# Three small vector operations of a two-branch attention layer go from VectorE to GpSimd

## The chip, the cores and the metric

One NeuronCore of one Trainium2 chip runs the whole kernel. The metric is the device time of one execution in microseconds (us); the lower, the better. The engines are named as the profile names them: PE (TensorE, matrix products), DVE (VectorE), ACT (ScalarE), POOL (GpSimd), SP (the queue that issues the transfers). Each engine works through its own queue in order; engines wait for one another by semaphores.

## What is computed

One encoder layer over a prompt of 2048 frames (and 8 running streams of 16 new frames with 512 cached ones). The rows are normalised and modulated, projected, and go through two attention branches; each branch's output is multiplied by a silu gate, projected, and both are merged. Branch A has 4 heads of differential attention (two softmaxes, the second subtracted with a factor lambda). Branch B has 8 heads of stick-breaking attention, whose weights are a sigmoid times a product of one minus the sigmoids of all later keys. The lines of the reference that the change bears on:

```python
# branch A
p = jax.nn.softmax(jnp.where(mask, s, -jnp.inf), axis=-1)
w = p[:, :, 0] - lam * p[:, :, 1]
# branch B
log_1m = jnp.where(mask, jax.nn.log_sigmoid(-z), 0.0)
log_a = jax.nn.log_sigmoid(z) + lax.cumsum(log_1m, axis=3, reverse=True) - log_1m
a = jnp.where(mask, jnp.exp(log_a), 0.0)
# both
ya = (oa.reshape(b, s, WIDTH_A) * jax.nn.silu(za)) @ w_branch_a
yb = (ob.reshape(b, s, WIDTH_B) * jax.nn.silu(zb)) @ w_branch_b
```

## The kernel before

The work has three stages. Up to about 150 us the inputs are normalised and modulated. Up to about 1745 us follow eight units, 0 to 7: for each of four pairs of heads a unit of branch A (the even ones) and a unit of branch B (the odd ones). After that come the branch outputs, the merge and the output projection, with the streams' attention between them.

A unit takes the 16 prompt tiles of 128 rows in turn, t = 0 to 15. `project` multiplies the tile with the unit's weights, some steps ahead of the attention; `scores` makes the scores of tile t against all keys up to it, in chunks of 512 columns, each in one PSUM bank of three (`ps_s`). The scores of a row lie in segments of at most 1024 keys, so a tile from t = 8 on has two segments. High-precision products are made of a high and a low half in 16 bits, so every operand is cut in two (`split`).

Branch B, per head and chunk, from the last chunk to the first: ACT makes two sigmoids (L135), one into the tile `sc_p` and one in place in the bank. DVE runs a multiplying scan from right to left over the bank into `sc_n` (`stick`, L675), each chunk beginning with the leftmost value of the chunk to its right. Where that chunk lies in the next segment (once for each head of a tile from t = 8 on), DVE first copies that value into the column behind the segment (L674) and the scan begins with the copy. POOL multiplies `sc_p` with `sc_n`, shifted by a column (`stick_weights`, L681), which is why that column must be there. Then `turn`: ACT casts the product to its high half (L609), DVE subtracts to get the low half (L612), and SP issues a transposing transfer into `wt` (L619), from which PE multiplies with the values (L762, L763), a set lag later. In unit 7 the turn follows at once; in the other units it is put off by a lag.

Silu of branch B's gate (`silu`, called at the start of `scores` of each tile): ACT makes the sigmoid of z into a tile of which there is one (`r2`), DVE multiplies z with it in place (L725). The result lies in a ring of eight (four in `szs`, four in `gt`) until POOL multiplies the head's output with it (`natural`, L745).

Branch A, per tile (`softmax_pair`): DVE takes the scores out of the bank with their maximum (L595), ACT makes the exponentials with their sums (L135), DVE works out factors from the sums (`sums`, L642 to L645): r[:,1] and r[:,2] for the join of both softmaxes (L650), and r[:,0], the common factor, which is scaled at L645 and is not needed before `turn` (ACT's cast L319 and DVE's subtraction L324). POOL applies the rotary embedding to branch A's projections (L507, L509, L512).

What comes when is settled twice: the program is written as interleaved pieces with lags, and a scheduler then orders each engine's queue by its own estimate of durations. So an operation that goes to another engine also moves others.

Of the kernel before, what the change touches and what calls it, by code (L numbers as in the profile page):

```python
# [22 lines left out]
ALU = mybir.AluOpType  # L23
# [102 lines left out]
def layer_kernel(ctx: ExitStack, tc: tile.TileContext, a: dict):  # L126
    nc = tc.nc
    V, S, G, T = nc.vector, nc.scalar, nc.gpsimd, nc.tensor
# [4 lines left out]
    def act(**kw):  # L133

        i = S.activation(**kw)  # L135
        if last_table[0] is not None:
            tc.add_manual_dep(i.ins, last_table[0].ins.name, NOSYNC, reason="table order")
        last_table[0] = i
        return i

    def kept(x):
        tc.keep_in_program_order(x)
        return x
# [68 lines left out]
    def bank(tag, dt=F32):  # L212
        return ps.tile([P, 512 if dt == F32 else 1024], dt, tag=tag, name=f"ps_{tag}", bufs=BANKS[tag])
# [114 lines left out]
    ls = ls_i.bitcast(F32)  # L328
# [244 lines left out]
    def new_job(U, t, c, nb, pool=None):  # L573

        segs = [(0, nb)] if t == NT else [(lo, min(lo + SEG, nb)) for lo in range(0, nb, SEG)]
        return dict(U=U, t=t, c=c, pool=pool, segs=[dict(lo=lo, hi=hi) for lo, hi in segs])
# [9 lines left out]
    def evacuate(job, seg, c, p, lo, n, sc_pos, sc_neg, ch):  # L586

        buffers(job, seg)
        if job["U"]["kind"] == 0:
            if "mx" not in job:  # L590
                job["mx"] = tiny.tile([P, 2, 4], F32, tag="mx", name="mx")
                job["nch"] = 0
            job["nch"] = max(job["nch"], ch + 1)
            dst = seg[("p", "n")[c]]
            V.tensor_scalar(out=dst[:, lo : lo + n], in0=p[:, 0:n], scalar1=sc_pos, scalar2=None,  # L595
                            op0=ALU.mult, op1=ALU.max, accum_out=job["mx"][:, c, ch : ch + 1])
        else:

            act(out=seg["p"][:, lo : lo + n], in_=p[:, 0:n], func=AF.Sigmoid, scale=sc_pos)
            act(out=p[:, 0:n], in_=p[:, 0:n], func=AF.Sigmoid, scale=sc_neg)  # L600

    def turn(job, seg, scale=None):

        nb = seg["hi"] - seg["lo"]
        nk = nb * P
        w16 = seg["n"].bitcast(F16)
        hi, lo, src = w16[:, 0:nk], w16[:, nk : 2 * nk], seg["p"][:, 0:nk]
        if scale is None:
            x = S.copy(out=hi, in_=src)  # L609
            if job["t"] < NT and job["U"]["u"] < 7:  # L610
                kept(x)
            V.tensor_tensor(out=lo, in0=src, in1=hi, op=ALU.subtract)  # L612
        else:
            split(hi, lo, src, scale, S)
        if job["t"] == NT:
            seg["wt"] = job["pool"].tile([P, 10, P], F16, tag="dwt", name="dwt", bufs=2)
        else:
            seg["wt"] = wtp.tile([P, 2 * SEG, P], F16, tag="wt", name="wt", bufs=WT_BUFS)
        nc.sync.dma_start_transpose(out=seg["wt"][:, 0 : 2 * nb, :], in_=w16[:, 0 : 2 * nk])  # L619
        if job["t"] < NT:  # L620
            cost = (PV_A, PV_B)[job["U"]["kind"]]
            for fn in pv(job, seg):
                later_on(PV_LAG, fn, cost)

    def softmax_pair(job):

        segs = job["segs"]
        nm = tiny.tile([P, 2], F32, tag="nm", name="nm")
        V.tensor_reduce(out=nm, in_=job["mx"][:, :, 0 : job["nch"]], axis=AX.X, op=ALU.max, negate=True)
        l = tiny.tile([P, 2, 2], F32, tag="l", name="l")  # L630
        r = tiny.tile([P, 3], F32, tag="r", name="r")
        n_all = sum(seg["hi"] - seg["lo"] for seg in segs) / SEG

        def powers(i, c):
            seg = segs[i]
            w = seg[("p", "n")[c]][:, 0 : (seg["hi"] - seg["lo"]) * P]
            act(out=w, in_=w, func=AF.Exp, bias=nm[:, c : c + 1], accum_out=l[:, c, i : i + 1])

        def sums():
            sums = l[:, :, 0]  # L640
            if len(segs) > 1:
                V.tensor_tensor(out=sums, in0=l[:, :, 0], in1=l[:, :, 1], op=ALU.add)  # L642
            V.reciprocal(out=r[:, 0:2], in_=sums)
            V.scalar_tensor_tensor(out=r[:, 2:3], in0=sums[:, 0:1], scalar=r[:, 1:2], in1=nlam, op0=ALU.mult, op1=ALU.mult)
            V.tensor_tensor(out=r[:, 0:1], in0=r[:, 0:1], in1=ls[:, 0:1], op=ALU.mult)  # L645

        def joined(seg):
            nk = (seg["hi"] - seg["lo"]) * P
            p, n = seg["p"][:, 0:nk], seg["n"][:, 0:nk]
            x = V.scalar_tensor_tensor(out=p, in0=n, scalar=r[:, 2:3], in1=p, op0=ALU.mult, op1=ALU.add)  # L650
            if job["t"] < NT:
                kept(x)

        stages = [(EXP_LAG, lambda i=i, c=c: powers(i, c)) for i in range(len(segs)) for c in range(2)]
        stages.append((EXP_LAG + SUM_LAG + 2.0 * n_all, sums))
        for i, seg in enumerate(segs):
            at = EXP_LAG + SUM_LAG + 2.0 * n_all + i
            stages += [(at, lambda seg=seg: joined(seg)), (at + TURN_LAG, lambda seg=seg: turn(job, seg, r[:, 0:1]))]
        for lag, fn in stages:
            if job["t"] == NT:  # L660
                fn()
            else:
                later_on(lag, fn)

    def stick(seg, later, lo, n, src):

        nk = (seg["hi"] - seg["lo"]) * P
        dst = seg["n"]
        if lo + n == nk and later is None:
            first = 2.0 ** STICK  # L670
        else:
            first = dst[:, lo + n : lo + n + 1]
            if lo + n == nk:
                V.tensor_copy(out=first, in_=later["n"][:, 0:1])  # L674
        V.tensor_tensor_scan(out=dst[:, lo : lo + n][:, ::-1], data0=src[:, 0:n][:, ::-1], data1=zero_t[:, 0:1].to_broadcast([P, n]),  # L675
                             initial=first, op0=ALU.mult, op1=ALU.add)

# [9 lines left out]
    def scores(U, t, jobs):  # L687

        sc, kind = U["sc"], U["kind"]
        nch = t // 4 + 1  # L690
        own = [new_job(U, t, c, t + 1) for c in range(1 + kind)]
        jobs += own

        def chunk(c, ch):
            job = own[c if kind == 1 else 0]
            seg = job["segs"][ch * 4 // SEG]
            n = 512 if ch < t // 4 else (t % 4 + 1) * P
            p = bank("s")
            qst, kk = U["q", t], U["k"][ch]
            diag = ch == t // 4  # L700
            T.matmul(p[:, 0:n], qst[:, c, :], kk[:, c, 0:n], start=True, stop=False)  # L701
            T.matmul(p[:, 0:n], qst[:, 2 + c, :], kk[:, c, 0:n], start=False, stop=not diag)  # L702
            if diag:
                m = mask_a if kind == 0 else mask_b
                T.matmul(p[:, n - m.shape[1] : n], idb, m, start=False, stop=True)  # L705
            evacuate(job, seg, c, p, ch * 512 - seg["lo"] * P, n, sc[:, 3:4], sc[:, 4:5], ch)
            if kind == 0:
                if diag and c == 1:
                    softmax_pair(job)
                return  # L710
            i = job["segs"].index(seg)
            later = job["segs"][i + 1] if i + 1 < len(job["segs"]) else None
            stick(seg, later, ch * 512 - seg["lo"] * P, n, p)
            if ch * 4 == seg["lo"]:
                if later is not None:
                    stick_weights(job, later, None)
                if i == 0:
                    stick_weights(job, seg, later)

        def silu():  # L720

            z = silu_z[t % len(rings)]
            sg = stg.tile([P, 256], F32, tag="r2", name="r2", bufs=1)[:, 0:P]
            act(out=sg, in_=z, func=AF.Sigmoid)
            V.tensor_tensor(out=z, in0=z, in1=sg, op=ALU.mult)  # L725

        order = [(c, ch) for ch in range(nch) for c in range(2)] if kind == 0 else \
                [(c, ch) for c in range(2) for ch in reversed(range(nch))]
        return ([(0.1, silu)] if kind == 1 else []) + [(2.0 if ch < t // 4 else (t % 4 + 1) / 2, lambda c=c, ch=ch: chunk(c, ch)) for c, ch in order]

    def natural(U, t, po, pool=stg):
# [35 lines left out]
    def later_on(lag, fn, cost=0.0):  # L767

        spent[1] += 1
        bisect.insort(due, (spent[0] + lag, spent[1], cost, fn))  # L770
# [276 lines left out]
    with tc.tile_pool(name="p0", bufs=1) as p0:  # L1047
# [28 lines left out]
        first = wide_tile().rearrange("p k n -> p (k n)")  # L1076
# [561 lines left out]
```

## Time and profile before

| what | us |
|---|---|
| median of 3 runs (lowest, highest) | 2212.37 (2209.06, 2217.97) |
| the profiled execution | 2207.3 |
| its span, first to last instruction | 2205.4 |
| PE busy | 2044.0 |
| DVE busy | 1734.5 |
| ACT busy | 1598.9 |
| POOL busy | 726.7 |

The profile is of one execution. Busy time is summed for each engine; a wait is put down to the instruction that ended it. A group has one line of the source, an engine, an operation and a shape, with busy time, mean duration in ns and the idle time ahead of it. A timeline has one instruction in a row: start and duration in us.

### The profile page before, as it was taken

To read this page: it belongs to the slowest core of one execution; us is meant where nothing else is said; L and a number is where in the kernel's file an instruction comes from. 1 tells how busy PE (TensorE), PEld (TensorE's weight loads), DVE (VectorE), ACT (ScalarE), POOL (GpSimd) and SP (SyncE) were. 2 spreads that over 40 slices of the span, in tenths; PEclk is the share of its full clock that TensorE was granted. 3 is DMA by queue.
4 is the path that set the end of the run, shared out by engine and by line. 5 is a ranking of instruction groups with operands and counts; after the bars stand their busy time and mean duration, and the time that the engine had idled before them with its cause. 6 is when DMAs were issued, how large, how long until landed. Compare 5 with 4: busy or idle time off the path is not lost. (4 is left out here: it accounts for less than half of the span.)

```text
span 2205.4 us, 40973 instructions
## 1 busy us (share of the span) xinstructions
PE 2044.0 (93%) x14504; PEld 1091.4 (49%) x14504; DVE 1734.5 (79%) x3651; ACT 1598.9 (72%) x3080; POOL 726.7 (33%) x618
## 2 busy tenths in 40 slices
PE   3999999999999999999999998999997799999997
PEld 1545555555555455555555545455554344444443
DVE  5668868889877887987878887787789778778874
ACT  3977677788877777978687788875687656666641
POOL 0433024466301444742034464402344412112220
PEclk9999999999999999999999999999999899999999
DMA  9778668899797999978888899885777899998862
GB/s 331 259 249 191 132 151 231 184 222 206 199 243 174 221 191 208 214 197 216 204 223 202 186 229 217 216 198 123 171 154 157 204 254 222 245 246 236 227 161 67
DMA packets 820814, 449.96 MB, mean 204 GB/s; under 512 B 551962, under 2 KB 759114, under 8 KB 820096
## 3 DMA queue, kind: packets, MB, share of 16 engines
q1 hardware_dynamic: 819660, 446.96, 82.1%
q8 instruction: 113, 1.85, 0.3%
q14 instruction: 93, 0.76, 0.1%
q10 hardware_dynamic: 948, 0.39, 0.1%
HBM read 229.87 MB, written 86.02 MB: 143 GB/s over the span
## 5 line engine op out<-in xcount | busy, mean ns | idle before, releaser
L681 POOL TENSOR_TENSOR sc_p<-sc_p,sc_n 128x127 f32<-128x127 f32 (+7 forms) x192 | 319.3, 1665 | 557.8 <-DVE sc_n L675 528.4
L466 PEld LDWEIGHTS <-hs 128*128 128x128 f16 x3120 | 292.8, 99 | 316.8 <-issue 9.1
L466 PE MATMUL ps_mm<-wa,hs 128*128 128x512 f16 x1590 | 390.5, 381 | 6.8 <-DMA hs<-hT_d 3.7
L466 PE MATMUL ps_mm<-wb,hs 128*128 128x512 f16 x1530 | 380.9, 380 | 0.0
L675 DVE TENSOR_TENSOR_SCAN sc_n<-ps_s,sc_n,zero_t 128x512 f32<-128x512 f32 x192 | 245.3, 1278 | 40.3 <-ACT ps_s L135 34.5
L612 DVE TENSOR_TENSOR sc_n<-sc_p,sc_n 128x128 f16<-128x128 f32 (+7 forms) x192 | 224.7, 1173 | 39.3 <-ACT sc_n L609 38.5
L701 PE MATMUL ps_s<-k,qst 128*128 128x512 f16 (+3 forms) x640 | 223.1, 349 | 32.2 <-DVE sc_n L675 27.8
L540 PEld LDWEIGHTS <-hs 128*128 128x128 f16 x1632 | 155.3, 98 | 184.2 <-DVE qst L569 4.8
L540 PE MATMUL ps_t<-wa,hs 128*128 128x512 f16 x1020 | 243.4, 381 | 1.1 <-DVE qst L569 0.7
L135 ACT ACTIVATE sc_p<-ps_s,usc 128x512 f32<-128x512 f32 (+3 forms) x320 | 205.7, 643 | 45.6 <-PE ps_s L702 34.2
L702 PE MATMUL ps_s<-k,qst 128*128 128x512 f16 (+3 forms) x640 | 223.1, 350 | 0.0
L609 ACT CAST sc_n<-sc_p 128x128 f16<-128x128 f32 (+7 forms) x192 | 155.9, 814 | 87.4 <-POOL sc_p L681 86.8
L135 ACT ACTIVATE ps_s<-ps_s,usc 128x512 f32<-128x512 f32 (+3 forms) x320 | 198.0, 619 | 0.0
L540 PE MATMUL ps_t<-wb,hs 128*128 128x512 f16 x612 | 150.5, 382 | 6.2 <-DMA hs<-hT_d 2.6
L1533 PE MATMUL ps_o<-wo,wb 128*128 128x512 f16 x672 | 151.1, 380 | 0.7 <-ACT wb L1307 0.7
L762 PE MATMUL ps_o<-v,wt 128*128 128x128 f16 x1088 | 133.1, 223 | 19.6 <-DMA wt<-sc_n 18.9
L1538 POOL TENSOR_TENSOR x<-m,x 128x512 f32<-128x512 f32 x32 | 45.9, 1434 | 249.5 <-DVE m L1536 174.1
L595 DVE TENSOR_SCALAR_CACHE_REDUCE sc_p<-ps_s,usc 128x512 f32<-128x512 f32 (+3 forms) x160 | 106.2, 664 | 24.1 <-PE ps_s L702 18.2
L763 PE MATMUL ps_o<-v,wt 128*128 128x64 f16 x1088 | 124.2, 195 | 0.0
L595 DVE TENSOR_SCALAR_CACHE_REDUCE sc_n<-ps_s,usc 128x512 f32<-128x512 f32 (+3 forms) x160 | 106.3, 664 | 22.7 <-PE ps_s L705 11.7
L762 PEld LDWEIGHTS <-wt 128*128 128x128 f16 x1088 | 100.1, 100 | 48.3 <-DMA wt<-sc_n 24.1
L1499 PEld LDWEIGHTS <-wa 128*128 128x128 f16 x816 | 77.9, 99 | 92.6 <-issue 7.8
(373 smaller groups left out, 4451.0 us busy)
## 6 DMA issues: line engine op xcount, KB each, us to landing
hs<-hT_d SPq DMA_DIRECT2D x132, 512.0 KB, 4.7
g_d<-gt SPq DMA_DIRECT2D x68, 256.0 KB, 4.0
out_dram<-pr SPq DMA_DIRECT2D x204, 64.0 KB, 3.9
o_d<-o SPq DMA_DIRECT2D x136, 64.0 KB, 3.2
wa<-g_d SPq DMA_DIRECT2D x17, 512.0 KB, 6.8
wb<-g_d SPq DMA_DIRECT2D x17, 512.0 KB, 5.3
hs<-o_d SPq DMA_DIRECT2D x17, 512.0 KB, 3.8
wide<-in_w_ada_dram SPq DMA_DIRECT2D x8, 1024.0 KB, 11.8
```

The source lines that it names most:

```text
L135: i = S.activation(**kw)
L466: T.matmul(box["p"], box["h"][:, hi, k, :], U["w"][k][:, wi, :], start=(n == 0), stop=(n == 3 * KT - 1))
L540: x = T.matmul(box["g"][:, 0:gw], box["h"][:, hi, k, :], U["wg"][k // per][:, k % per, wi, :], start=(j == 0), stop=(j == 3 * KT - 1))
L595: V.tensor_scalar(out=dst[:, lo : lo + n], in0=p[:, 0:n], scalar1=sc_pos, scalar2=None, op0=ALU.mult, op1=ALU.max, accum_out=job["mx"][:, ...
L609: x = S.copy(out=hi, in_=src)
L612: V.tensor_tensor(out=lo, in0=src, in1=hi, op=ALU.subtract)
L675: V.tensor_tensor_scan(out=dst[:, lo : lo + n][:, ::-1], data0=src[:, 0:n][:, ::-1], data1=zero_t[:, 0:1].to_broadcast([P, n]), initial=fi ...
L681: G.tensor_tensor(out=p[:, 0:m], in0=p[:, 0:m], in1=n[:, 1 : m + 1], op=ALU.mult)
L701: T.matmul(p[:, 0:n], qst[:, c, :], kk[:, c, 0:n], start=True, stop=False)
L702: T.matmul(p[:, 0:n], qst[:, 2 + c, :], kk[:, c, 0:n], start=False, stop=not diag)
L762: T.matmul(po[:, c * P : (c + 1) * P], wt[:, wj, :], vt[:, c, :, :], start=first, stop=False)
L1533: T.matmul(po, st["y"][:, yi * 8 + k, :], wo[j * 4 + k // 2][:, wi, k % 2, :], start=(n == 0), stop=(n == 3 * KT - 1))
```

## The change

Three operations go from DVE to POOL: the scaling of branch A's factor r[:,0] (68 times, once for each tile of each unit of branch A), the copy of the carried column (64 times) and silu's product (64 times). The copy is still made, since `stick_weights` reads the column, but the scan no longer begins with it: it reads the next segment's leftmost value itself. One line is added, so lines from L675 on are one higher in the changed kernel.

```diff
@@ sums, in softmax_pair
-            V.tensor_tensor(out=r[:, 0:1], in0=r[:, 0:1], in1=ls[:, 0:1], op=ALU.mult)
+            G.tensor_tensor(out=r[:, 0:1], in0=r[:, 0:1], in1=ls[:, 0:1], op=ALU.mult)
@@ stick
             if lo + n == nk:
-                V.tensor_copy(out=first, in_=later["n"][:, 0:1])
+                G.tensor_copy(out=first, in_=later["n"][:, 0:1])
+                first = later["n"][:, 0:1]
         V.tensor_tensor_scan(out=dst[:, lo : lo + n][:, ::-1], data0=src[:, 0:n][:, ::-1], data1=zero_t[:, 0:1].to_broadcast([P, n]),
                              initial=first, op0=ALU.mult, op1=ALU.add)
@@ silu
-            V.tensor_tensor(out=z, in0=z, in1=sg, op=ALU.mult)
+            G.tensor_tensor(out=z, in0=z, in1=sg, op=ALU.mult)
```

POOL's queue in unit 7 (branch B) near its end, before: stick products of the tiles t = 13 and 14 (the width tells the segment: 1024 the lower one, 767 and 895 the upper one) and the gate products L745.

```order
L681 TENSOR_TENSOR sc_p<-sc_p,sc_n 128x767
L681 TENSOR_TENSOR sc_p<-sc_p,sc_n 128x1024
L681 TENSOR_TENSOR sc_p<-sc_p,sc_n 128x767
L681 TENSOR_TENSOR sc_p<-sc_p,sc_n 128x1024
L681 TENSOR_TENSOR sc_p<-sc_p,sc_n 128x895
L745 TENSOR_TENSOR o<-o,gt_1396 128x128
```

The same place now, where L682 is the stick product, L746 the gate product, L674 the carried column and L726 silu's product:

```order
L682 TENSOR_TENSOR sc_p<-sc_p,sc_n 128x767
L682 TENSOR_TENSOR sc_p<-sc_p,sc_n 128x1024
L674 COPY sc_n<-sc_n 128x1
L682 TENSOR_TENSOR sc_p<-sc_p,sc_n 128x767
L746 TENSOR_TENSOR o<-o,gt_1396 128x128
L726 TENSOR_TENSOR gt_1396<-gt_1396,r_21529 128x128
L682 TENSOR_TENSOR sc_p<-sc_p,sc_n 128x1024
L674 COPY sc_n<-sc_n 128x1
L682 TENSOR_TENSOR sc_p<-sc_p,sc_n 128x895
```

Each head's carried column stands ahead of its upper product, and the next tile's silu stands between the last two products of a tile.

ACT's queue at the same place, before: casts (L609), pairs of sigmoids (L135) and the sigmoid of silu, into `r`.

```order
L135 ACTIVATE r_21529<-gt_1396 128x128
L609 CAST sc_n<-sc_p 128x1024
L609 CAST sc_n<-sc_p 128x768
L135 ACTIVATE sc_p<-ps_s,usc_18672 128x384
L135 ACTIVATE ps_s<-ps_s,usc_18672 128x384
L545 ACTIVATE gt_1396<-ps_t,usc_18672 128x512
```

And now:

```order
L609 CAST sc_n<-sc_p 128x1024
L609 CAST sc_n<-sc_p 128x768
L135 ACTIVATE sc_p<-ps_s,usc_18672 128x512
L135 ACTIVATE ps_s<-ps_s,usc_18672 128x512
L135 ACTIVATE r_21529<-gt_1396 128x128
L135 ACTIVATE sc_p<-ps_s,usc_18672 128x384
L135 ACTIVATE ps_s<-ps_s,usc_18672 128x384
```

The sigmoid of silu has moved behind the two casts and a pair of sigmoids; for the neighbouring tiles it stands as it did.

POOL's queue in unit 4 (branch A), before: the rotary embedding of the projections, three operations a tile.

```order
L507 TENSOR_TENSOR rot<-pr,rope 128x256
L509 TENSOR_TENSOR r_12426<-pr,rope 128x256
L512 TENSOR_TENSOR rot<-rot,r_12426 128x256
L507 TENSOR_TENSOR rot<-pr,rope 128x256
L509 TENSOR_TENSOR r_12556<-pr,rope 128x256
```

And now, with the factor of branch A's weights (L645):

```order
L507 TENSOR_TENSOR rot<-pr,rope 128x256
L509 TENSOR_TENSOR r_12426<-pr,rope 128x256
L512 TENSOR_TENSOR rot<-rot,r_12426 128x256
L645 TENSOR_TENSOR r<-r,ls_i 128x1
L507 TENSOR_TENSOR rot<-pr,rope 128x256
L509 TENSOR_TENSOR r_12556<-pr,rope 128x256
```

A factor stands between the groups of two tiles, behind a whole group.

## The prediction

> **What bounds the kernel now.** I read the engines' busy time first, then the waits of each engine, then the busy time of each stage, and last the timeline of the one stage in which TensorE does worst.
>
> ```profile
> PE 2044.0 (93%) x14504; PEld 1091.4 (49%) x14504; DVE 1734.5 (79%) x3651; ACT 1598.9 (72%) x3080; POOL 726.7 (33%) x618
> ```
>
> TensorE (PE) is busy for 2044.0 of 2205.4 us, so whatever VectorE (DVE) is spared can return at most the 161 us in which PE waits. Busy time by stage: 290 to 530 us is unit 1 (branch B), 530 to 690 is unit 2 (branch A), the last two rows are the two halves of unit 7 (branch B).
>
> ```profile
> core 0: us, PE busy (x) PEld busy (x) DVE busy (x) ACT busy (x) POOL busy (x), PEclk, DMA share, GB/s
> 1510.00:1640.00 130.00, 126.10 (x878) 67.91 (x877) 101.12 (x179) 93.35 (x195) 45.55 (x38) 1.00 0.69 157
> 1640.00:1745.00 105.00, 78.88 (x622) 43.25 (x620) 95.39 (x108) 77.59 (x135) 56.47 (x32) 0.93 0.75 157
> ...
> 290.00:530.00 240.00, 235.38 (x1714) 128.55 (x1712) 203.31 (x328) 201.24 (x402) 117.10 (x93) 1.00 0.86 201
> 530.00:690.00 160.00, 152.88 (x1084) 84.64 (x1082) 129.91 (x345) 120.23 (x259) 39.56 (x41) 1.00 0.81 205
> ```
>
> In three of these PE is the limit (95 to 98% busy). Only from 1640 to 1745 us does it fall to 75%, and there DVE is at 91%: that stretch is DVE's. The waits of PE from 290 to 1760 us say the same (us in total, times, longest); the fourth row is the first one's share in 1640 to 1745.
>
> ```profile
> PE ps_s L701 <- DVE sc_n L675: 27.8, 31, 2.4
> PE ps_o L762 <- DMA wt<-sc_n: 18.9, 15, 3.2
> PE ps_o L758 <- DMA wt<-sc_n: 9.4, 8, 2.2
> ```
> ```profile
> PE ps_s L701 <- DVE sc_n L675: 14.8, 17, 2.4
> ```
>
> PE waits 27.8 us for a bank of scores that a scan still reads, 14.8 of them in DVE's stretch and 13.0 elsewhere, and 28.3 us for turned weights (`wt`). Fewer DVE instructions can shorten the first; a later GpSimd (POOL) can lengthen the second.
>
> **What leaves DVE.** The three groups (busy us, mean ns), and the spread of one of them:
>
> ```profile
> L725 DVE TENSOR_TENSOR gt<-gt,r 128x128 f32<-128x128 f32 x32 | 19.3, 602 | 0.0
> L725 DVE TENSOR_TENSOR szs<-szs,r 128x128 f32<-128x128 f32 x32 | 12.7, 396 | 5.0 <-ACT r L135 5.0
> L645 DVE TENSOR_TENSOR r<-r,ls_i 128x1 f32<-128x1 f32 x68 | 10.3, 152 | 0.0
> L674 DVE COPY sc_n<-sc_n 128x1 f32<-128x1 f32 x64 | 9.6, 150 | 4.5 <-DMA wt<-sc_n 3.0
> ```
> ```profile
> L725 DVE TENSOR_TENSOR gt<-gt,r x32: 258/266/2090, 322.2 to 1716.1; 128x128 f32<-128x128 f32 x32
> ```
>
> 32.0 + 10.3 + 9.6 = 51.9 us, 3% of DVE's 1734.5. The silu products should cost 64 x 0.266 = 17 us by their median; the other 15 are products held up to 2.09 us. Where that comes from shows in DVE's and POOL's timelines inside the stretch (start, us):
>
> ```profile
> 1680.62 0.27 DVE L725 TENSOR_TENSOR gt<-gt,r 128x128 f32<-128x128 f32 x1
> 1680.80 1.22 DVE L612 TENSOR_TENSOR sc_n<-sc_p,sc_n 128x1024 f16<-128x1024 f32 x1
> ...
> 1684.48 1.27 DVE L675 TENSOR_TENSOR_SCAN sc_n<-ps_s,sc_n,zero_t 128x512 f32<-128x512 f32 x1
> 1685.78 0.15 DVE L674 COPY sc_n<-sc_n 128x1 f32<-128x1 f32 x1
> 1685.86 2.60 DVE L612 TENSOR_TENSOR sc_n<-sc_p,sc_n 128x1024 f16<-128x1024 f32 x1
> ```
> ```profile
> 1683.84 1.03 POOL L745 TENSOR_TENSOR o<-o,szs 128x128 f32<-128x128 f32 x1
> 1685.83 1.54 POOL L681 TENSOR_TENSOR sc_p<-sc_p,sc_n 128x767 f32<-128x767 f32 x1 [0.96 <-DVE sc_n L675]
> ```
>
> The same subtraction takes 1.22 us at 1680.80 and 2.60 at 1685.86, 0.03 us after a POOL product had started: 1.38 us more, about what that product lasts. So a DVE operation with two SBUF inputs stands still while POOL works. The Trainium skill (SBUF — State Buffer, "Who interferes with whom") says this: DVE with two SBUF inputs and a POOL operation that reads SBUF exclude each other for the whole instruction. These rows agree.
>
> In the stretch, which the DVE rows bound directly, this leaves:
>
> ```profile
> L674 DVE COPY sc_n<-sc_n 128x1 f32<-128x1 f32 x10 | 1.5, 149 | 0.2
> L725 DVE TENSOR_TENSOR gt<-gt,r 128x128 f32<-128x128 f32 x4 | 1.1, 266 | 0.0
> L725 DVE TENSOR_TENSOR szs<-szs,r 128x128 f32<-128x128 f32 x1 | 0.3, 257 | 0.0
> ```
>
> Instructions overlap at their ends, so a slot is less than a duration. A silu holds DVE from 1680.62 to 1680.80: 0.18 us. The copy waits out the scan (1685.75), and the next instruction starts at 1685.86 where it could have started about 0.08 before the scan's end: 0.19 us. So 5 x 0.18 + 10 x 0.19 = 2.8 us. Nothing else takes their place there at once, since DVE is the engine that is late.
>
> Elsewhere the removed time is hidden behind PE, apart from the 13.0 us of scan waits. A unit of branch B loses (32.0 - 1.4 + 9.6 - 1.5) / 4 = 9.7 us of about 203 DVE us, 5%; the waits are the tail of DVE's delay and react more strongly than its mean. I take a quarter, 3.0 us; the ends are 0 and 13. The factor (L645) I count at nothing: in branch A's stage DVE is 81% busy and PE 96%, so PE covers it; uncovered it would be worth 10.3 us at most. The scan's new start value costs nothing: it waits for the previous scan on its own engine either way.
>
> **What POOL gets.** The same 128x128 product is there already (L745); for one column only a memset is:
>
> ```profile
> L745 POOL TENSOR_TENSOR o<-o,szs 128x128 f32<-128x128 f32 x32 | 23.0, 721 | 20.8 <-issue 8.0 <-DVE usc L409 6.9 <-DVE o L743 5.1
> L745 POOL TENSOR_TENSOR o<-o,gt 128x128 f32<-128x128 f32 x32 | 20.7, 648 | 47.9 <-DVE o L743 27.9 <-DMA x<-in_w_out_dram 9.7 <-DVE r L643 6.8
> L1626 POOL MEMSET const-float32-1.0<- 128x1 f32 x1 | 0.1, 98 | 0.0
> ```
>
> 64 silus at (721 + 648) / 2 = 0.68 us are 44 us. The 132 one-column operations cost between 0.10 (the memset) and 0.65 us each, 13 to 86 us; I take 0.15, near the memset, since there is next to no data: 20 us. POOL goes from 727 to about 790 us, 36%: no bound. What matters is its order. A silu waits for ScalarE's (ACT's) sigmoid, and behind it in POOL's queue stands a stick product (L681), whose cast ACT awaits in order:
>
> ```profile
> 1695.26 1.54 POOL L681 TENSOR_TENSOR sc_p<-sc_p,sc_n 128x767 f32<-128x767 f32 x1 [2.15 <-DVE sc_n L675]
> ...
> 1698.22 3.03 POOL L681 TENSOR_TENSOR sc_p<-sc_p,sc_n 128x1024 f32<-128x1024 f32 x1 [1.42 <-DVE sc_n L675]
> ```
> ```profile
> 1694.02 0.33 ACT L135 ACTIVATE r<-gt 128x128 f32<-128x128 f32 x1
> ...
> 1696.84 0.83 ACT L609 CAST sc_n<-sc_p 128x768 f16<-128x768 f32 x1 [1.55 <-POOL sc_p L681]
> ```
>
> With today's times the sigmoid is done at 1694.35, so the silu fits the gaps between products; where the new order puts the sigmoid behind the cast it delays one product by about 2 us. One such place shows in the order of the stretch; I charge 1.0 us, as DVE has other scans to do meanwhile (without that cover 2 us, and 5 tiles x 2 = 10 us if every late tile had it).
>
> Sum: -2.8 - 3.0 + 1.0 = -4.8 us. The profiled execution took 2207.3 us and would take 2202.5; it lies 5 us under the median of the runs, 2212.4, so the forecast for the median is 2207.6 us.
>
> **Rivals.** *DVE's relief counts in full.* If all 13.0 us of scan waits outside the stretch go, the sum is -2.8 - 13.0 = -16 us: 2196. For it: 15 us of the silus' time on DVE is standing still, in the units where the waits are. Against it: PE is 97 to 98% busy there, and each wait that goes uncovers another. Chance 0.23.
>
> *The exclusion eats it.* The silu, now on POOL, stops DVE's subtractions instead of being stopped. It saves 0.266 us of DVE and occupies POOL for 0.68; a blocked subtraction loses on average half of that, 0.34, as often as one is due. If the two balance, and the stretch's 2.8 us go into the 2 us of the late product, the time is unchanged: 2212. The Trainium skill (Perfetto Trace Analysis, "Optimizing Scalar/DVE Operations") speaks against the change so: moving work between DVE and POOL might not help, because they share a port. The trace bears out the port, not the balance. Chance 0.13.
>
> *The factor comes late (slower).* In branch A, r[:,0:1] now leaves POOL behind the three rope products of a projection, while ACT's cast (L319) waits for it. Today that cast waits for the join (L650):
>
> ```profile
> L512 POOL TENSOR_TENSOR rot<-rot,r 128x256 f32<-128x256 f32 x68 | 66.5, 978 | 5.2
> L509 POOL TENSOR_TENSOR r<-pr,rope 128x256 f32<-128x256 f32 x68 | 62.2, 915 | 30.9 <-issue 15.2 <-ACT pr L480 12.3 <-DMA o_d<-o 1.2
> L507 POOL TENSOR_TENSOR rot<-pr,rope 128x256 f32<-128x256 f32 x68 | 60.3, 886 | 162.8 <-ACT pr L480 73.8 <-DVE qkbuf L501 31.2 <-DVE r L644 15.1
> ```
> ```profile
> L650 DVE SCALAR_TENSOR_TENSOR sc_p<-sc_n,r,sc_p 128x1024 f32<-128x1024 f32 x40 | 52.8, 1323 | 0.0
> ```
>
> A whole rope group is 978 + 915 + 886 = 2.78 us, the join hides 1.32 of it, and 1.46 us would pass to the cast, the transposes behind it and PE's 9.4 us of waits for `wt` at L758. It decides the sign from (4.8 + 11) / 1.46 = 11 late factors among the 64 prompt tiles; at 12 the time is 2212.4 - 4.8 + 12 x 1.46 = 2225. For it: the order puts each factor right behind a rope group. Against it: POOL is 25% busy in that stage, and the products with `wt` come a long lag after the turn. Chance 0.19.
>
> That the change doesn't do what it says I exclude: the diff names the engine in all three places.
>
> **How the numbers follow.** Forecast (a gain of some 5 us) 0.45, full relief 0.23, no change 0.13, late factors 0.19. About 0.5%, 11 us, is what a measurement of this kernel can tell from no change. Full relief and 0.02 of the forecast's spread lie beyond it below: faster 0.25. Late factors and 0.02 lie beyond it above: slower 0.21. The rest, 0.54, is the same. The likeliest case is 2207.6; its own range is 2199 to 2214. The range for 8 in 10 reaches from full relief, 2195, to the late factors, 2225.
>
> **What would show it.** Right: silu (L726 there, one line lower) and L674 on POOL at 0.5 to 1.0 and about 0.15 us; DVE busy 50 us less; PE's wait for scans falling from 27.8 to some 22 us, with DVE in the last stretch still the busiest. Wrong on the small size: those waits under 15 us. Wrong on the sign: PE's waits for `wt` above 40 us in place of 28.3, ACT's L319 waiting for POOL's L645, or DVE's L612 longer in the mean.

## The result and the profile after

The changed kernel takes 2221.6 us (median of 20 runs, 2215.3 to 2231.2), the kernel before 2213.5 (20 runs, 2203.7 to 2220.4). The ratio is 1.0037, 95% interval 1.0024 to 1.0049: 8 us slower where a gain of 5 was forecast: inside the forecast's range but on the other side of no change. The profiled execution took 2218.0 us with a span of 2215.9; before it was 2207.3 and 2205.4.

What the prediction said of the engines' busy times went the way it said. First the page's busy times of the changed kernel, then its GpSimd (POOL) groups (busy us, mean ns, idle before). From L675 on, its lines are one higher than in before.

```profile
PE 2054.9 (93%) x14504; PEld 1094.6 (49%) x14504; DVE 1695.2 (76%) x3455; ACT 1595.3 (72%) x3080; POOL 785.3 (35%) x814
```
```profile
L674 POOL COPY sc_n<-sc_n 128x1 f32<-128x1 f32 x64 | 26.1, 408 | 64.0 <-DVE sc_n L676 61.9 <-DMA wt<-sc_n 2.1
L726 POOL TENSOR_TENSOR gt<-gt,r 128x128 f32<-128x128 f32 x32 | 19.3, 604 | 31.1 <-ACT r L135 29.2 <-DVE csc L947 1.9
L726 POOL TENSOR_TENSOR szs<-szs,r 128x128 f32<-128x128 f32 x32 | 17.2, 537 | 97.4 <-ACT r L135 97.4
L645 POOL TENSOR_TENSOR r<-r,ls_i 128x1 f32<-128x1 f32 x68 | 16.4, 242 | 292.3 <-DVE r L643 259.1 <-DMA s_d<-v 11.0 <-DVE cexp L946 8.2
```

POOL gains 58.6 us where 64 were forecast; VectorE (DVE) loses 39.3 where 52 were. TensorE's (PE) waits from 290 to 1760 us, in the changed kernel, and then the scan waits from 1640 to 1745 alone:

```profile
PE ps_s L702 <- DVE sc_n L676: 21.9, 25, 2.3
PE ps_o L763 <- DMA wt<-sc_n: 20.3, 15, 3.5
PE ps_o L759 <- DMA wt<-sc_n: 12.6, 10, 2.2
PE ps_mm L466 <- DMA hs<-hT_d: 9.4, 4, 3.6
```
```profile
PE ps_s L702 <- DVE sc_n L676: 7.9, 9, 2.3
```

The scan waits fell from 27.8 to 21.9 us, as forecast, and the waits for turned weights rose from 28.3 to 32.9, under the 40 that was to tell of late factors. New is the last row of four: PE waits for `hs`, the tile of h that the projection multiplies. To find where the 10 us went I set the two traces side by side and compared when the k-th matmul starts. The changed kernel is 0.4 us late at the 2100th (352 us), 7.4 at the 2400th (397), 10.1 at the 3000th (486), and from there to the end between 5 and 13. So in this execution the whole loss is made in unit 1, between 350 and 490 us. PE's waits from 340 to 600 us, before and after:

```profile
PE ps_s L701 <- DVE sc_n L675: 3.6, 5, 1.5
PE ps_o L762 <- DMA wt<-sc_n: 2.3, 2, 1.3
PE ps_mm L466 <- DVE v L324: 0.7, 1, 0.7
```
```profile
PE ps_mm L466 <- DMA hs<-hT_d: 5.9, 3, 3.1
PE ps_s L702 <- DVE sc_n L676: 4.9, 6, 2.0
PE ps_mm L466 <- DVE v L324: 2.8, 1, 2.8
```

That is 13.6 us against 6.6. The other 3 us are PE's clock, which the last section shows. The three waits for `hs` in PE's timeline of the changed kernel (start, duration, what it waited for):

```profile
349.44 4.28 PE L466 MATMUL ps_mm<-wb,hs 128*128 128x512 f16 x19 [1.03 <-DMA hs<-hT_d]
366.30 5.65 PE L466 MATMUL ps_mm<-wb,hs 128*128 128x512 f16 x19 [3.13 <-DMA hs<-hT_d]
383.77 3.20 PE L466 MATMUL ps_mm<-wb,hs 128*128 128x512 f16 x14 [1.70 <-DMA hs<-hT_d]
```

The middle one is for tile 10. SyncE's (SP) timeline shows its load, first in before, then in after. The pair of stores L520 and L521, which writes out projected rows and waits for ScalarE (ACT), and one store of `o_d` stood behind this load and now stand ahead of it; the two transposes stand ahead of it in both kernels and go out later now.

```profile
354.77 0.40 SPq L443 DMA_DIRECT2D hs<-hT_d  x1
357.20 1.58 SPq L619 DMA_TRANSPOSE wt<-sc_n  x1
358.87 1.07 SPq L520 DMA_DIRECT2D out_dram<-pr  x1
```
```profile
347.84 0.34 SPq L520 DMA_DIRECT2D out_dram<-pr  x1
...
355.08 4.71 SPq L619 DMA_TRANSPOSE wt<-sc_n  x2
359.88 0.53 SPq L933 DMA_DIRECT2D wb<-in_cache_a_k_dram  x1
360.47 0.57 SPq L753 DMA_DIRECT2D o_d<-o  x1
361.13 0.39 SPq L443 DMA_DIRECT2D hs<-hT_d  x1
```

SP takes its queue in order, so the load that was issued at 354.77 us goes out at 361.13. What holds the queue up from 290 to 410 us, of SP's own waits, before and then after:

```profile
SPq L520 <- ACT pr L484: 6.3, 4, 2.9
...
SPq L619 <- DVE sc_n L612: 3.3, 4, 1.7
```
```profile
SPq L520 <- ACT pr L484: 14.8, 6, 8.8
SPq L619 <- DVE sc_n L676: 9.9, 4, 4.7
SPq L619 <- DVE sc_n L612: 9.3, 4, 4.7
```

Of the 14.8 us for ACT, one wait of 8.8 us ends at 297 us, before the loss begins; from 340 to 410 us this row has 4.8 us, in before 0.9. Nothing in these rows is work on GpSimd. **Theory 1 (order):** the scheduler, given the moved operations, ordered unit 1 in another way on all engines, and that order costs the time. Its rivals: **theory 2**, GpSimd's own queue delays products, columns and silus everywhere; **theory 3**, the factor comes late to ACT's cast L319, as in the forecast's slower case. In the programs, the change leaves 511 of ACT's 2624 instructions and 299 of SP's 1498 at another place in the sequence that both kernels share.

### The profile page after: what moved, and what is told of

The parts are those of the page before. It is cut to its first block, busy times and chain, and to the rows that moved or that the text cites. A ratio compares the mean times of both kernels' runs of the same rounds, so it can differ in the third digit from the quotient of the medians.

```text
span 2215.9 us, 40964 instructions
## 1 busy us (share of the span) xinstructions
PE 2054.9 (93%) x14504; PEld 1094.6 (49%) x14504; DVE 1695.2 (76%) x3455; ACT 1595.3 (72%) x3080; POOL 785.3 (35%) x814
## 5 line engine op out<-in xcount | busy, mean ns | idle before, releaser
L682 POOL TENSOR_TENSOR sc_p<-sc_p,sc_n 128x127 f32<-128x127 f32 (+7 forms) x192 | 302.8, 1577 | 223.8 <-DVE sc_n L676 185.3
L612 DVE TENSOR_TENSOR sc_n<-sc_p,sc_n 128x128 f16<-128x128 f32 (+7 forms) x192 | 231.5, 1209 | 41.6 <-ACT sc_n L609 41.3
L135 ACT ACTIVATE sc_p<-ps_s,usc 128x512 f32<-128x512 f32 (+3 forms) x320 | 206.0, 644 | 59.1 <-PE ps_s L703 38.8
L702 PE MATMUL ps_s<-k,qst 128*128 128x512 f16 (+3 forms) x640 | 223.1, 349 | 26.3 <-DVE sc_n L676 21.9
L609 ACT CAST sc_n<-sc_p 128x128 f16<-128x128 f32 (+7 forms) x192 | 156.3, 818 | 74.4 <-POOL sc_p L682 70.1
L135 ACT ACTIVATE ps_s<-ps_s,usc 128x512 f32<-128x512 f32 (+3 forms) x320 | 198.2, 619 | 0.0
L676 DVE TENSOR_TENSOR_SCAN sc_n<-ps_s,zero_t 128x128 f32<-128x128 f32 (+3 forms) x128 | 104.1, 814 | 29.2 <-ACT ps_s L135 28.3
```

Source lines behind the costliest of these rows:

```text
L682: G.tensor_tensor(out=p[:, 0:m], in0=p[:, 0:m], in1=n[:, 1 : m + 1], op=ALU.mult)
```

## The experiments

Times against the kernel before, 5 rounds on the same chip as runs of before (4 to 12 executions of each); 1 thousandth is 2.2 us.

| run | ratio, 95% interval | us |
|---|---|---|
| e1: factor on POOL in unit 0 | 1.0021 (1.0000 to 1.0042) | +4.6 |
| e2: the change without that factor | 0.9975 (0.9958 to 0.9993) | -5.5 |
| e3: the change, unit 1's loads first | 1.0007 (0.9990 to 1.0024) | +1.5 |
| e4: the change without any factor | 0.9993 (0.9978 to 1.0008) | -1.5 |
| e5: before, five loads late | 1.0005 (0.9993 to 1.0018) | +1.1 |
| e6: the change in unit 7 alone | 0.9966 (0.9950 to 0.9982) | -7.5 |
| e7: silu's product alone | 1.0023 (1.0009 to 1.0037) | +5.1 |
| e8: factor in units 2, 4, 6 alone | 1.0093 (1.0072 to 1.0115) | +21 |
| e9: e8's arithmetic, before's order | 1.0007 (0.9991 to 1.0023) | +1.5 |
| e10: before's arithmetic, e8's order | 1.0112 (1.0092 to 1.0131) | +25 |
| e11: before's arithmetic, the change's order | 1.0053 (1.0034 to 1.0072) | +12 |
| e12: the change's arithmetic, e2's order | 0.9986 (0.9973 to 0.9999) | -3.1 |
| e13: before, SP alone in the change's order | 1.0378 (1.0356 to 1.0400) | +84 |
| e14: silu's product, unit 7 alone | 0.9997 (0.9982 to 1.0012) | -0.7 |
| e15: column and scan, unit 7 alone | 0.9979 (0.9965 to 0.9993) | -4.6 |
| e16: before's arithmetic, e6's order | 0.9997 (0.9981 to 1.0012) | -0.7 |
| e17: before's arithmetic, e2's order | 1.0010 (0.9995 to 1.0026) | +2.2 |

**Which part of the change moves the loads (e1 to e4).** The change puts seven of unit 1's loads of `hs` behind one to three more transposes each; one edit alone, the factor in unit 0, does that to six of them. So e1 has only that, on the kernel before:

```diff
-            V.tensor_tensor(out=r[:, 0:1], in0=r[:, 0:1], in1=ls[:, 0:1], op=ALU.mult)
+            (G if job["U"]["u"] == 0 else V).tensor_tensor(out=r[:, 0:1], in0=r[:, 0:1], in1=ls[:, 0:1], op=ALU.mult)
```

> The kernel before with one edit: the factor of branch A's weights (L645) is made by GpSimd in unit 0 alone (16 or 17 one-column operations of some 0.2 us); silu, the scan's column and all other units stay as before. Theory 1 (order): this factor alone makes the scheduler put seven or eight of unit 1's loads of the next h tile behind one to three more weight transposes in SyncE's queue, and that is where the changed kernel loses its time; so +6 to +10 us against before, PE waits of 1 to 3 us each for hs<-hT_d between 340 and 410 us, and all of the drift there. Theory 2 (GpSimd's queue delays products and columns everywhere): nothing that counts is added here, so 0 within 2 us. Theory 3 (the factor comes late to ACT's L319): a quarter of the branch A units, so a quarter of the loss, +2 us, with L319 waiting for GpSimd.

e2 is the changed kernel with only this undone:

```diff
-            G.tensor_tensor(out=r[:, 0:1], in0=r[:, 0:1], in1=ls[:, 0:1], op=ALU.mult)
+            (G if job["U"]["u"] else V).tensor_tensor(out=r[:, 0:1], in0=r[:, 0:1], in1=ls[:, 0:1], op=ALU.mult)
```

> The changed kernel with one edit: unit 0 makes its factor on VectorE as before, all the rest of the change stays (silu, column, scan, factor in units 2, 4 and 6). Theory 1 (order): unit 1's loads of the h tiles go back to their places, so the loss goes and the forecast's two gains remain: -2 to -5 us against before, half-clock time back near 71 us. Theory 2 (GpSimd's queue): nearly all of its work stays, so the loss stays: +6 to +9 us. Theory 3 (late factor): three quarters of the loss, +5 to +7 us.

e3 keeps the whole change and ties the transposes behind the loads (`HS_AT` holds, per tile, how many transposes stood ahead of its load in before):

```diff
...
-        load(out=ahead[u, t], in_=hT_d[t // 4][:, t % 4, :, :, :])
+        x = load(out=ahead[u, t], in_=hT_d[t // 4][:, t % 4, :, :, :])
+        if u == 1:
+            for y in wt_loads[HS_AT.get(t, len(wt_loads)) :]:
+                tc.add_manual_dep(y.ins, x.ins.name, NOSYNC, reason="load first")
...
```

> The changed kernel with all of its GpSimd work, and one thing more: in unit 1 the weight transposes that stood behind a load of the next h tile in the kernel before are tied to come after it in SyncE's queue again; nothing else is ordered by hand. Theory 1 (order): the loads' places cost the time, not the arithmetic, so -1 to -5 us against before, and no PE wait over 1 us for hs<-hT_d between 340 and 410 us. Theory 2 (GpSimd's queue): +6 to +9 us, as the change. Theory 3 (late factor): +6 to +9 us. If unit 1 loses its time to the rest of the new order (ACT's above all) and not to the loads, +4 to +9 us with no wait for hs<-hT_d.

e4 is the change with L645 on `V` in all units.

> The changed kernel without the factor's move: silu's product, the column's copy and the scan's input as changed, the factor on VectorE in all units. Theory 1 (order): unit 1's loads stay at their places, so -2 to -5 us against before, as the run without unit 0's factor, since the factor was costed at nothing elsewhere. Theory 2 (GpSimd's queue, silu and columns held up by one another): +6 to +9 us. Theory 3 (late factor): the loss goes, -2 to -5 us, as theory 1; the two are told apart by the run with the factor in unit 0 alone and the one without it there.

Seventeen one-column operations in unit 0 decide the sign: with them the change costs 8 us, without them (e2) it gains 5.5. By themselves (e1) they cost about 5, less than theory 1's 6 to 10 and with an interval that begins at 0; PE waited for `hs` in unit 1 only once, 0.9 us, and more than half of the loss in e1's profiled execution comes after 1510 us. In e2 the half-clock time did not go back to 71 us either, it was 88. Theory 2 had +6 to +9 us for e2, which keeps nearly all of GpSimd's work, and falls. (That the seventeen last only 4 us together, 0.24 us each, would not be enough: one that waits at the head of a queue also holds what stands behind it, as in SP's rows above. e12 below puts them back.) Theory 3 had five to seven us of loss for e2 and falls too; in the changed kernel ACT's casts L319 wait so (us, times, longest):

```profile
ACT sc_n L319 <- DVE sc_p L650: 33.5, 27, 2.7
...
ACT sc_n L319 <- POOL r L645: 1.1, 2, 0.8
```

e3 brings back 6.5 of the 8 us with all of GpSimd's work in place, less than theory 1's -1 to -5 against before, and leaves no wait for `hs` from 340 to 410 us. e4 lies between e2 and before and is not told apart from either; theory 1 had -2 to -5 for it.

**Are the loads themselves the cost (e5), and the other parts (e6 to e8).** e5 is the kernel before with the reverse of e3: five loads tied behind the transposes that the changed kernel has ahead of them.

```diff
+    wt_loads, BEHIND = {}, {5: (0, 14), 7: (1, 1), 8: (1, 2), 9: (1, 4), 11: (1, 6)}
...
+        if u == 1 and t in BEHIND:
+            for y in wt_loads[BEHIND[t]]:
+                tc.add_manual_dep(x.ins, y.ins.name, NOSYNC, reason="load later")
...
```

> The kernel before, all arithmetic on its old engines; only five of unit 1's loads of the h tile (for tiles 5, 7, 8, 9 and 11) are tied to come behind the weight transposes that the changed kernel has ahead of them in SyncE's queue (one to three more). Theory 1 (order): the loads' places alone cost about half of what separates the changed kernel from the one without unit 0's factor, +4 to +8 us against before, with PE waits for hs<-hT_d of 4 to 7 us between 340 and 410 us. Rival (the loads are only a symptom, and the time goes to something else in the new order of unit 1, ACT's sequence or the half clock): 0 to +2 us, even if PE waits there.

+1.1 us, and from 200 to 600 us PE waited for `hs` once, 0.9 us, in place of the 4 to 7 us expected; the rival had it right. So theory 1 in its narrow form, that more transposes ahead of the loads cost the time, fell. e5 does not bring back the whole of the loads' places: the stores L520 and L521 stand ahead of eleven loads in the changed kernel that they stood behind before, and ahead of two in e5. e6 has `if U["u"] == 7` around each of the change's three edits (the factor's never applies, as unit 7 is of branch B), e7 only the silu edit, e8 only L645 with `G if job["U"]["u"] else V`.

> The change in unit 7 alone: silu's product and the column on GpSimd, the scan reading the next segment's column; units 0 to 6 as before. By the forecast's first term (the DVE-bound stretch of unit 7): -2 to -4 us against before, nothing earlier than 1640 us. If GpSimd's queue eats it (its products behind other work there): -1 to +1 us. If the gains of the run without unit 0's factor came from elsewhere (the scan waits of units 1, 3 and 5): 0 to -1 us.

> The kernel before with silu's product alone on GpSimd; column, scan and factor as before. Here the scheduler puts six to eight loads of the h tile in each of units 3 and 5 behind one to four more transposes. Theory 1 (order): that costs as in unit 1 of the changed kernel, though there are two such units, so +3 to +12 us, with PE waits for hs<-hT_d in units 3 and 5 and none in unit 1. Theory 2 (GpSimd's queue): the product's own price, -2 to +1 us.

> The kernel before with the factor on GpSimd in units 2, 4 and 6 and not in unit 0. Theory 1 (order): only two loads in each of units 3 and 5 go two transposes back, so 0 to +4 us. Theory 3 (the factor itself comes late to ACT): three quarters of the loss, +5 to +7 us, with L319 waiting for GpSimd in all three units. By the forecast (a factor costs nothing): 0 within 2 us.

e6, the change where the prediction saw the gain, has the lowest median of the study, 2205.7 us, and beats both before and the changed kernel; e2, e12 and e15 lie within its error. e7 lost 5 us by the order theory's sign, but its waits for `hs` were not where I had expected them: none in units 3 and 5, 5.7 us in unit 7. e8 was a surprise to all theories: 51 one-column operations, 21 us.

**Order and arithmetic apart (e9 to e12).** Instructions keep their names in all these kernels, so one kernel's arithmetic can be given the other's order: each engine's instructions are chained, without any semaphore, in the other kernel's sequence. Only operations that changed their engine find their place freely. `ORDER` is that sequence, packed:

```python
    made = {i.name: i for i in nc.cur_bb.bb.instructions}
    for row in zlib.decompress(base64.b85decode(packed)).decode().split(";"):
        ...
            if last is not None and last.engine == i.engine:
                tc.add_manual_dep(i, last.name, NOSYNC, reason="other order")
```
```diff
         layer_kernel(tc, aps)
+        in_order_of(tc, nc, ORDER)
```

> The arithmetic of the run with the factor on GpSimd in units 2, 4 and 6 (9 thousandths slower than before), but every engine is tied to take its instructions in the order of the kernel before; only GpSimd's new one-column operations find their place freely. Order theory (the time went to the new order that the scheduler made around the factor): 0 within 3 us of before. Engine theory (a factor on GpSimd reaches ACT too late, or holds GpSimd's queue): +15 to +21 us, as in the free order.

> The reverse: all arithmetic as in the kernel before, the factor on VectorE, but every engine in the order that the scheduler made for the factor on GpSimd in units 2, 4 and 6. Order theory: +15 to +22 us against before with nothing at all moved to GpSimd. Engine theory: 0 within 3 us.

> All arithmetic as in the kernel before, every engine in the order of the changed kernel. Order theory: the changed kernel's order without its arithmetic's gain of about 5.5 us, so +9 to +14 us against before. Engine theory (GpSimd's work is what costs): 0 within 3 us. If order and arithmetic go together (the order fits the moved work and suits the old work worse): more than +14 us.

> The whole change, unit 0's factor on GpSimd too, with every engine in the order of the run that kept unit 0's factor on VectorE. Order theory: as that run, -3 to -8 us against before. Engine theory (unit 0's 17 factors on GpSimd cost the 13 us themselves): +6 to +10 us, as the change.

In the traces of e9 to e12 each of the five engines takes the instructions that both kernels have on it in exactly the order that was given. All four came out as the order theory had them (e10 a little above it). The factors that cost 21 us cost 1.5 in the old order (e9); their order alone, with nothing moved to GpSimd, costs 25 (e10). Both e8 and e10 lose 15 us of it between 1510 and 1640 us, by the matmuls' starts, and there PE waits 7.0 and 7.9 us for `hs`, in before and e9 not at all. The changed kernel's order with the old arithmetic costs 12 (e11), and the whole change in e2's order gains 3.1 (e12). e11 has not one operation of the change; these are its busy times, PE's waits from 340 to 600 us, PE's timeline and SP's:

```profile
PE 2051.7 (92%) x14504; PEld 1094.2 (49%) x14504; DVE 1727.1 (78%) x3651; ACT 1594.7 (72%) x3080; POOL 723.6 (33%) x618
```
```profile
PE ps_s L701 <- DVE sc_n L675: 6.2, 5, 3.0
PE ps_mm L466 <- DMA hs<-hT_d: 5.3, 3, 2.6
```
```profile
353.40 4.28 PE L466 MATMUL ps_mm<-wb,hs 128*128 128x512 f16 x19 [1.01 <-DMA hs<-hT_d]
369.72 4.28 PE L466 MATMUL ps_mm<-wb,hs 128*128 128x512 f16 x19 [2.58 <-DMA hs<-hT_d]
385.79 3.19 PE L466 MATMUL ps_mm<-wb,hs 128*128 128x512 f16 x14 [1.74 <-DMA hs<-hT_d]
```
```profile
358.96 4.81 SPq L619 DMA_TRANSPOSE wt<-sc_n  x2
363.86 0.53 SPq L932 DMA_DIRECT2D wb<-in_cache_a_k_dram  x1
364.45 0.57 SPq L752 DMA_DIRECT2D o_d<-o  x1
365.11 0.38 SPq L443 DMA_DIRECT2D hs<-hT_d  x1
```

Four us later, because this execution lost them earlier, it is the changed kernel's stretch again, row for row; by the matmuls' starts e11 is 3.5 us behind before at 340 us and 16.7 at 530. In e12, with all of the change's work on GpSimd, the waits for `hs` in the same window are all but gone:

```profile
PE ps_mm L466 <- DMA hs<-hT_d: 0.2, 1, 0.2
```

The reverse, the whole change in the order of before, was not tried, because it cannot run: the scan now reads the first column of the next segment itself, the cast L609 overwrites that column, and in ACT's old order some of these casts stand ahead of the sigmoid that this scan needs.

**Which engine's order (e13).** The chaining again, with SP's row from the changed kernel and the other four rows from before.

> All arithmetic as in the kernel before, and four engines in its order; SyncE alone takes its transfers in the order of the changed kernel, from start to end. Queue theory (the changed order costs by the places of the transfers in SyncE's queue): +9 to +13 us against before, as the run with every engine in the changed order. Rival (the order of TensorE, ScalarE and VectorE costs, and SyncE's only follows it): 0 to +4 us, with PE waits for hs<-hT_d under 2 us between 340 and 410 us.

+84 us, more than six times what either theory allowed: from 310 to 440 us SP waited 41.0 us for ACT's projections (L520 on L484), where in before it waits 3.8. Here a queue out of step with the engines cost 84 us where the same order on all of them costs 12 (e11), so this run says nothing on which engine's order costs the 12 us.

**What unit 7 gained (e14 to e17).** e14 and e15 split e6 into the silu edit and the column edit; e16 and e17 chain the old arithmetic into the orders of e6 and e2.

> The kernel before with silu's product on GpSimd in unit 7 alone. If products and columns gain in unit 7 as the forecast split them (0.9 to 1.9): a third of the 7.5 us that unit 7 gave, -1.5 to -3.5 us. If the column alone does it, since it stands in the chain from scan to scan: 0 within 1.5 us.

> The kernel before with the column's copy on GpSimd and the scan reading the next segment's column in unit 7 alone; silu's product stays on VectorE. By the forecast's split: -3 to -5.5 us. If the column alone does it: -6 to -9 us. If it is silu's product: 0 within 1.5 us.

> All arithmetic as in the kernel before, every engine in the order that the scheduler made for the change in unit 7 alone (which was 7.5 us faster than before). If the copies and products themselves held VectorE up: 0 to -1.5 us, the gain is gone. If the gain came with the new order of unit 7: -6 to -9 us with nothing moved to GpSimd. Between the two, each has its share.

> All arithmetic as in the kernel before, every engine in the order of the run that kept unit 0's factor on VectorE (5.5 us faster than before). If the moved work itself gains: 0 to +2 us. If the order gains: -4 to -7 us.

By the medians the column carries it (-4.6 against -0.7), but each has an error of some 3 us, so the two are not told apart. With the order held, the old arithmetic is slower than the new by 6.8 us (e16 against e6), by 7.7 (e17 against e2) and by some 4 (e11 against the changed kernel), each within some 5 us. So the moved work itself is worth some 4 to 8 us, clear of noise in the first two pairs. Where it is won is less clear. PE's scan waits from 1640 to 1745 us are lower with the new arithmetic in all three pairs (9.6 us against 12.4, 7.5 against 12.5, 7.9 against 11.6), in one execution each. But by the matmuls' starts e6 gains 4.2 us on before from 1630 to 1756 us in its profiled execution, and e16 and e11, with the old arithmetic, 3.1 and 5.2, and e9, in before's own order, 2.3: before's profiled execution was slow there.

## Why the prediction was wrong

**Where it failed.** The step is "The factor (L645) I count at nothing". It is right about the engines: POOL makes a factor in 0.24 us, ACT waits 1.1 us for factors in all, and in the old order three quarters of them cost 1.5 us within an error of 3.5 (e9). But the move of an instruction was costed only by the work and the waits of that instruction. The prediction looked at the new order in unit 7 and at POOL's queue in branch A, and took everything else to stand where it stood, though the description of the kernel says that a moved operation also moves others. It did not stand: unit 0's factors turn a gain of 5.5 us (e2) into a loss of 8, since they lead the scheduler to another order, and the changed kernel's order costs 12 us with the old arithmetic (e11), in unit 1 as far as the profiled executions show. Against these 12 stands the moved work; what is left of the +8 gives -4 for it; the two other pairs gave -6.8 and -7.7. No term of the forecast's sum stood for the order.

**VectorE's freed slots, -2.8 us.** The wait was right: unit 7's scan waits went from 14.8 to 7.9 us. The size was too small, since e6 gave 7.5 (3.9 to 11). The split, 0.9 for the products and 1.9 for the columns, stands beside 0.7 and 4.6 (e14, e15) with errors of some 3 us, so it is neither shown nor refuted.

**The quarter of the scan waits elsewhere, -3.0 us.** Against before this did not happen. From 500 to 1640 us, before and after:

```profile
PE ps_s L701 <- DVE sc_n L675: 10.4, 11, 1.5
```
```profile
PE ps_s L702 <- DVE sc_n L676: 11.4, 12, 2.0
```

The total fell to "some 22" as forecast, but all of it in unit 7: a sum that agrees does not bear out its parts. The new order hides something here. With the order held, the scan waits outside that stretch do fall, from 20.0 us (e11) to 14.0 (the changed kernel) and from 20.4 (e17) to 15.5 (e2). In the same pairs PE's waits for `wt` rise, from 22.5 to 32.9 and from 23.7 to 27.1, so a wait that goes uncovers another, as the rival of full relief was told.

**The late product, +1.0 us.** POOL does stand idle for the silus' sigmoids (126.6 us in the two L726 rows above), yet ACT's casts wait less for products than before: 70.1 us in place of 86.8, and in the stretch 5.3 in place of 13.2. The charge was not needed; e11 has 5.9 there with nothing moved, so the new order made the difference.

**The rivals.** Late factors had the right sign by the wrong mechanism: ACT's L319 waited for POOL's L645 twice, 1.1 us in all. For the exclusion of DVE and POOL, the subtraction L612 was to grow; here in before, in after and in e11:

```profile
L612 DVE TENSOR_TENSOR sc_n<-sc_p,sc_n 128x128 f16<-128x128 f32 (+7 forms) x192 | 224.7, 1173 | 39.3 <-ACT sc_n L609 38.5
```
```profile
L612 DVE TENSOR_TENSOR sc_n<-sc_p,sc_n 128x128 f16<-128x128 f32 (+7 forms) x192 | 231.5, 1209 | 41.6 <-ACT sc_n L609 41.3
```
```profile
L612 DVE TENSOR_TENSOR sc_n<-sc_p,sc_n 128x128 f16<-128x128 f32 (+7 forms) x192 | 236.3, 1234 | 32.0 <-ACT sc_n L609 31.6
```

It is 36 ns longer in the mean after the change, but 61 ns longer in e11, which has the same order and none of the moved work. So the growth goes with the order, and no run here shows that the silus on POOL slow the subtractions. Where the 12.6 us went that DVE did not get back is not shown. No rival named the order of the other engines. (In the prediction's table by stage the halves of unit 7 are the first two rows, not the last two; its readings of them are right.)

**What stays open.** Which part of the order costs the 12 us. One trait goes with the loss in the traces. The stores L520 and L521, which wait for ACT's projection, stand ahead of nine to thirteen loads of `hs` that they stood behind in before, in each of the kernels that are 4.6 us or more slower (the changed one, e1, e7, e8, e10, e11, e13). In e2, e6, e9, e12 and e14 to e17, which lie between -7.5 and +2.2 us, they do so for none. SP's waits for ACT's projection at L520 agree in part: 4.8 us from 340 to 410 us in the changed kernel and 5.5 in e11, 0.9 in before; 20.7 from 1510 to 1640 us in e8 and 20.6 in e10, 8.4 in before; but e1 has only 0.7 from 340 to 410. And no run moves these stores alone. e3 has them ahead of nine loads without the extra transposes and is 4.6 us slower than e12, which has the same arithmetic, within an error of about that size; e4 has the stores ahead of three loads (-1.5), e5 of two, with five loads behind extra transposes (+1.1). So the cause within the order is argued and not shown.

## What to carry to other kernels

Where a scheduler orders the queues, an edit has two prices, that of the work it moves and that of the order it sets off, and here the second was the larger (-0.7 to +25 us, for four of the scheduler's orders with the same arithmetic). So compare the sequences of all engines over the whole program before costing an edit, look first for loads that fall behind stores or transposes that wait for an engine, and make the edit only where it pays (unit 7 alone: -7.5 us). To tell the two prices apart, run the old arithmetic in the new order.

## What the hardware showed

**Half a window can be enough to lose the clock.** The granted clock (third figure from the end, columns as in the prediction's table by stage) in stretches of 3.4 us, in the changed kernel around the second wait for `hs`:

```profile
358.90:362.30 3.40, 3.40 (x35) 2.28 (x34) 2.31 (x4) 3.34 (x7) 1.21 (x1) 1.00 0.86 182
362.30:365.70 3.40, 0.88 (x13) 0.54 (x10) 2.96 (x9) 3.40 (x11) 1.99 (x3) 1.00 1.06 366
365.70:369.10 3.40, 2.80 (x7) 1.03 (x8) 3.40 (x4) 1.23 (x3) 3.11 (x3) 0.50 1.10 269
369.10:372.50 3.40, 3.40 (x17) 1.53 (x16) 1.84 (x3) 0.00 (x0) 1.11 (x2) 1.00 0.47 80
```

PE was busy 0.88 of 3.40 us, and for the next 3.40 us its clock is 0.50. In these PE was busy 2.80 us, so by estimate about 1.4 us are lost on top of the wait. The same happened once more in unit 1, at 488.6 us, for 1.7 us, and the two make up the 3 us that the waits left over:

```profile
485.20:488.60 3.40, 1.66 (x16) 0.98 (x16) 3.31 (x4) 3.29 (x8) 2.72 (x5) 1.00 1.12 247
488.60:492.00 3.40, 3.40 (x22) 1.82 (x20) 3.40 (x4) 3.40 (x7) 3.07 (x3) 0.50 1.07 222
```

The Trainium skill (TensorE: Matmul & The Clock Gate, Part 1) says that the gate watches a free-running window of 3413 ns and passes either all pulses or half of them; the records agree in both (0.50 or 1.00, and the two dips lie 122.9 us apart, 36 times 3.414). The same page of the Trainium skill (Why this matters for your kernels) advises against idle gaps of over some 3 us. By these rows that is too mild: ahead of 488.6 us PE was still busy for 1.66 of 3.40 us, and its two longest waits were 1.3 and 0.7. It is no sharp limit: from 734.4 to 737.8 us PE was busy for 1.47 of 3.40 us, and the clock stayed at 1.00. So waits of 2 us can cost nearly 4, or only themselves.

**Executions differ with it.** Over its 20 runs the changed kernel's mean clock was 0.9787, that of 35 runs of before 0.9801; a thousandth of clock goes with 1.2 to 1.7 us in either kernel's runs. So some 2 of the 8 us go with the clock, and the clock of one profiled execution (0.978 against 0.984) exaggerates it.

**GpSimd's small operations.** One column of 128 values took 0.24 us (L645) and 0.41 us (L674) in the mean, 0.19 in either's median, against 0.15 on DVE, and the 128x128 product 0.54 to 0.60 us; I had taken 0.15 and 0.68.
